# One masked product per group of tiles, and beta by ScalarE: the inverse of a gated DeltaNet layer

## The chip, the cores and the metric

The kernel runs on one core of one Trainium2 chip. The metric is the device time of one execution in microseconds (us); of several runs the median counts. In the profile PE is TensorE, the matmul engine (PEld its weight loads), DVE is VectorE, ACT is ScalarE, POOL is GpSimd, and SP is SyncE, which issues DMAs.

## What is computed

Two layers of a trunk run over 640 tokens: a gated MLP (layer A) and then a bidirectional gated DeltaNet (layer B) with 8 heads of 128 key and 256 value channels. The change is in layer B. Cut to what matters, for a head and a direction:

```python
diff  = gcum[..., :, None] - gcum[..., None, :]
decay = jnp.exp(jnp.where(tril_incl, diff, -jnp.inf))
kb    = kc * bc[..., None]                       # bc is beta, one number per token
A     = jnp.where(tril_strict, einsum('bnhid,bnhjd->bnhij', kb, kc) * decay, 0.0)
lhs   = A + jnp.eye(CHUNK_B)
sol   = triangular_solve(lhs, rhs, left_side=True, lower=True)
qk    = jnp.where(tril_incl, einsum('bnhid,bnhjd->bnhij', qc, kc) * decay, 0.0)
...
v_new = u_i - w_i @ S                            # scan over the chunks
o     = qd_i @ S + qk_i @ v_new
S     = S * gl_i + kd_i.T @ v_new
```

So A is the decayed Gram matrix of the keys, times beta of a row, under a strict triangular mask; the unit matrix plus A is inverted. The query-key matrix with its inclusive mask is multiplied with the solution. Both are done once forward and once backward, and the two directions differ in their triangular masks and in beta.

## The kernel before

Layer B takes the 640 tokens as 5 tiles of 128 (tile 0 the context, tiles 1 to 4 the latents), and its chunk is a tile of 128. The inverse is made by `chunk`, for one head and one group of tiles at a time: `GROUPS = (0,), (1, 4), (2, 3)`, so nt is 1, 2 and 2. There are 8 heads, 24 calls, 40 tiles, and 80 pairs of a tile and a direction.

A call of `chunk` does this. L964 multiplies keys and queries with the keys on PE into a PSUM bank; L967 and L969 (DVE) multiply by the decay `ex`, into g (`ge` in the profile) and pe. L974 makes A: for each tile and direction one DVE operation on 128x128 elements, g times beta (one number per partition) times the strict mask m[0] or m[1]. After the next `yield` L982 makes two of the four parts of M in the same way, from pe and the inclusive masks m[2] and m[3]; L985 (ACT) writes the key parts of M, `kn` scaled by one number per partition. L988 and L990 (POOL) split A plus the unit matrix into two 16-bit halves, A16 and L16; L1002 (PE) turns A16, L1004 (DVE) and L1005 (POOL) write the first level of the inverse into the tile TU; then come six levels (L1017 PE, L1022 DVE, L1028 and L1029 PE, L1032 ACT), a step that refines the inverse (L1047 to L1066), and L1073 (PE) multiplies M by it. L1075 (ACT) copies the product into G, which the scan of this head reads later (L1125, L1126).

A and M have one buffer for each nt. Group (2,3) therefore writes M only when L1073 of group (1,4) has read its own, and that is shortly before its own L1073, when the kernel goes over from one head's scan to the next.

The work of a head is cut into parts (projection, convolution, z gate, `scan`, `chunk` of the next head, norm, residual), each a generator that is advanced from `yield` to `yield` in the order of due times (`stages`, `turns`). With `tc.manual_schedule(engines=MANUAL)` PE and SP keep the order in which this writes their instructions. On DVE, ACT and POOL the order is the scheduler's. Every engine runs its own queue in order: one that waits holds all behind it.

Around the change stand, on the same engines: the short convolution of the next head, L845 (ACT), four L848 (DVE), tanh L851 (ACT), L853 (DVE), and then L240 (PE), which transposes its result into the one PSUM bank of kind `px` that L938 (ACT) reads out and frees; the z gate L1199 (ACT) and L1200 (DVE), which free a bank of kind `pp`; the scan L1112 (PE), L1115 (DVE), L1118 (ACT), L1131 and L1138 (ACT), L1140 (DVE), which adds up the output o and frees a bank of kind `ps` that L1112 fills next; and the split of weights into two parts, L230 (ACT) and L231 (POOL or DVE). PSUM banks: pp 2, pt 3, px 1, ps 2.

Of the kernel before, what the change touches and what calls it, by code (L numbers as in the profile page):

```python
# [9 lines left out]
AF = mybir.ActivationFunctionType  # L10
ALU = mybir.AluOpType
PSUM = bass.MemoryType.PSUM

P = 128
# [193 lines left out]
class Trunk:  # L208
# [8 lines left out]
    def t(self, pool, shape, dt, tag, bufs=None):  # L217
        kw = {} if bufs is None else {"bufs": bufs}
        return pool.tile(shape, dt, tag=tag, name=self.name(tag), **kw)
# [724 lines left out]
    def chunk(self, h, cs):  # L944


        nc, a, t = self.nc, self.a, self.t
        b1, b2 = self.b1, self.b2
        m = self.masks
        kq = self.kq[h]  # L950
        nt = len(cs)
# [3 lines left out]
        two_each = lambda ap: ap[:, :, None, :].broadcast_to([P, 2, nt, P])  # L955
# [10 lines left out]
        g = t(b1, [P, nt, P], F32, f"ge{nt}", bufs=AB[nt - 1])  # L966
        nc.vector.tensor_tensor(g, pg[:, 0], self.ex[:, those], op=ALU.mult)  # L967
        pe = t(b1, [P, nt, P], F32, f"pe{nt}")
        nc.vector.tensor_tensor(pe, pg[:, 1], self.ex[:, those], op=ALU.mult)  # L969

        A = t(b1, [P, 2, nt, P], F32, f"A{nt}", bufs=AB[nt - 1])
        for i, c in enumerate(cs):
            for d in range(2):
                nc.vector.scalar_tensor_tensor(A[:, 1 - d, i], g[:, i], self.beta[:, c, d, h : h + 1], m[:, 1 - d],  # L974
                                               op0=ALU.mult, op1=ALU.mult)

        M = t(b1, [P, nt, 4, P], F32, f"M{nt}")
        keys = lambda c, d: c == 0 or c != (4, 1)[d]
        yield
        for i, c in enumerate(cs):  # L980
            for d in range(2):
                nc.vector.scalar_tensor_tensor(M[:, i, 1 + d], pe[:, i], self.beta[:, c, d, h : h + 1], m[:, 2 + d],  # L982
                                               op0=ALU.mult, op1=ALU.mult)
                if keys(c, d):
                    nc.scalar.activation(M[:, i, 3 * d], kn[:, i], AF.Copy, scale=self.scal[:, 2 + d, c, h : h + 1])  # L985
        yield
        A16 = t(b1, [P, 2, nt, P], F16, f"A16{nt}", bufs=A16B[nt - 1])
        nc.gpsimd.tensor_tensor(A16, A, self.ident[:, None, None, :].broadcast_to([P, 2, nt, P]), op=ALU.add)  # L988
        L16 = t(b1, [P, 2, nt, P], F16, f"L16{nt}", bufs=A16B[nt - 1])
        nc.gpsimd.tensor_tensor(L16, A, A16, op=ALU.subtract)  # L990
        yield
# [429 lines left out]
```

## Time and profile before

| | before |
|---|---|
| median of 3 runs | 1355.61 us (1353.62 to 1361.57) |
| profiled execution, its own time | 1356.03 us |
| its span | 1354.2 us |
| granted TensorE clock, mean | 0.99 |
| layer A | 0 to about 540 us |
| layer B, projection of the first head to the last scan | about 540 to 1240 us |
| output of layer B | about 1240 to 1354 us |

The span is what the profiler saw between the first and the last instruction. A line such as `L974 DVE ... A<-ge,beta,masks 128x128 ... x80 | 28.6, 415 | 0.0` tells line 974, engine, operation, what is written from what, partitions by elements, how many, then their busy time in us, the mean of one in ns, and the engine's idle time just ahead of them. In a timeline the row begins with start and duration in us, and the bracket at its end is the idle time ahead of it and who ended it. A waits row gives total, times and the longest in us.

### The profile page before, as it was taken

Reading aid. Unit: us, or ns where it says so; the run is one execution under the profiler, and the core shown is the slowest. Engines: PE = TensorE matmul, PEld = TensorE weight load, DVE = VectorE, ACT = ScalarE, POOL = GpSimd, SP = SyncE. Lnnn points to the kernel's source line nnn. Section 1 sums busy time; section 2 is a strip of 40 time slices with the busy share of each in tenths; the row PEclk is TensorE's granted clock in tenths of the full one; section 3 lists DMA queues with packets and bytes.
Section 4 is the critical chain, followed back from the end, with each engine's and each line's share of the span. In section 5 each row is a group of like instructions: output and inputs, shape, how many; then the busy total and the mean of one; then the engine's idle time right before and its main releaser. Section 6 shows DMA issues by size and latency. Waiting matters only on the chain. (4 is left out here: it accounts for less than half of the span.)

```text
span 1354.2 us, 22812 instructions
## 1 busy us (share of the span) xinstructions
PE 1282.5 (95%) x8773; PEld 1137.3 (84%) x8773; DVE 875.7 (65%) x1655; ACT 578.7 (43%) x1352; POOL 502.0 (37%) x503
## 2 busy tenths in 40 slices
PE   7999999999999999888999999999999999999996
PEld 4688999999997887778888898999899898887785
DVE  4654744444447566798677778686787868656357
ACT  2333522222224334665545354564545546443320
POOL 0221422222223434354343536355464646520024
PEclk9999999999999999998999999999999999999999
DMA  8512233333336324142122422234233242445732
GB/s 337 168 63 93 94 125 125 125 125 125 125 125 218 118 76 145 56 140 86 50 77 73 136 78 65 100 89 153 79 125 108 85 139 88 133 141 174 261 117 78
DMA packets 90254, 163.17 MB, mean 120 GB/s; under 512 B 9089, under 2 KB 55457, under 8 KB 90017
## 3 DMA queue, kind: packets, MB, share of 16 engines
q1 hardware_dynamic: 88704, 156.99, 35.3%
q10 hardware_dynamic: 1440, 4.72, 1.0%
q8 instruction: 69, 1.13, 0.3%
q14 instruction: 41, 0.33, 0.1%
HBM read 135.97 MB, written 25.71 MB: 119 GB/s over the span
## 5 line engine op out<-in xcount | busy, mean ns | idle before, releaser
L231 POOL TENSOR_TENSOR wlo<-wraw,whi 128x256 fp32r<-128x256 f32 (+1 forms) x188 | 194.4, 1054 | 261.6 <-ACT whi L230 261.6
L235 PE MATMUL pp<-hThi,whi 128*128 128x320 f32 (+1 forms) x784 | 280.1, 357 | 0.2 <-ACT hThi L230 0.2
L237 PE MATMUL pp<-hTlo,whi 128*128 128x320 f32 (+1 forms) x784 | 244.7, 312 | 0.4 <-POOL hTlo L231 0.4
L236 PE MATMUL pp<-hThi,wlo 128*128 128x320 f32 (+1 forms) x784 | 244.1, 311 | 0.0
L230 ACT CAST whi<-wraw 128x256 fp32r<-128x256 f32 (+1 forms) x262 | 143.5, 593 | 84.6 <-PE pacc L236 57.6
L235 PE MATMUL pacc<-hThi,whi 128*128 128x320 f32 x512 | 159.6, 312 | 0.0
L237 PE MATMUL pacc<-hTlo,whi 128*128 128x320 f32 x512 | 158.3, 309 | 0.0
L236 PE MATMUL pacc<-hThi,wlo 128*128 128x320 f32 x512 | 158.2, 309 | 0.0
L848 DVE SCALAR_TENSOR_TENSOR cacc<-xp,convw,cacc 128x642 f32<-128x642 f32 x128 | 137.7, 1076 | 25.0 <-ACT cacc L845 23.6
L235 PEld LDWEIGHTS pp<-hThi,whi 128*128 128x128 f32 (+1 forms) x784 | 148.8, 190 | 3.9 <-ACT hThi L230 0.3
L236 PEld LDWEIGHTS pp<-hThi,wlo 128*128 128x128 f32 (+1 forms) x784 | 148.6, 190 | 4.0
L237 PEld LDWEIGHTS pp<-hTlo,whi 128*128 128x128 f32 (+1 forms) x784 | 147.7, 188 | 1.8 <-POOL hTlo L231 0.7
L231 DVE TENSOR_TENSOR wlo<-wraw,whi 128x1024 fp32r<-128x1024 f32 (+1 forms) x74 | 87.7, 1196 | 60.0 <-ACT whi L230 59.5
L248 POOL TENSOR_TENSOR rs<-ve,mhalf 128x1 f32<-128x1 f32 (+2 forms) x39 | 40.1, 1028 | 170.1 <-DVE ve L246 166.7
L235 PEld LDWEIGHTS pacc<-hThi,whi 128*128 128x128 f32 x512 | 96.1, 188 | 3.1 <-issue 2.2
L236 PEld LDWEIGHTS pacc<-hThi,wlo 128*128 128x128 f32 x512 | 96.1, 188 | 0.0
L237 PEld LDWEIGHTS pacc<-hTlo,whi 128*128 128x128 f32 x512 | 96.1, 188 | 0.0
L256 POOL TENSOR_SCALAR gsq<-gsq 128x320 f32<-128x320 f32 (+1 forms) x52 | 27.7, 532 | 138.4 <-ACT gsq L255 137.4
L257 DVE TENSOR_TENSOR gsq<-pacc,gsq 128x320 f32<-128x320 f32 (+1 forms) x52 | 29.1, 565 | 73.9 <-POOL gsq L256 73.8
L255 ACT ACTIVATE gsq<-pacc 128x320 f32<-128x320 f32 (+1 forms) x52 | 25.7, 498 | 106.2 <-PE pacc L237 102.3
L235 PE MATMUL pacc<-whi,hThi 128*128 128x512 f32 x160 | 63.1, 406 | 7.6 <-ACT whi L230 4.4
L1032 ACT CAST TU<-pt 128x512 f16<-128x512 f32 (+1 forms) x120 | 57.2, 525 | 26.4 <-PE pt L1029 25.5
(333 smaller groups left out, 2974.9 us busy)
## 6 DMA issues: line engine op xcount, KB each, us to landing
wraw<-in_w_b SPq DMA_DIRECT2D x48, 512.0 KB
wraw<-in_w_ada SPq DMA_DIRECT2D x37, 512.0 KB
wraw<-in_w_uz SPq DMA_DIRECT2D x32, 512.0 KB
v<-kvd SPq DMA_DIRECT2D x72, 128.0 KB
wraw<-in_a_wo SPq DMA_DIRECT2D x16, 512.0 KB
wraw<-in_b_wo SPq DMA_DIRECT2D x16, 512.0 KB
kvd<-nat SPq DMA_DIRECT2D x24, 320.0 KB
cacc<-yd SPq DMA_DIRECT2D x24, 320.0 KB
```

The lines of the kernel that those rows point to most:

```text
L230: self.nc.scalar.copy(hi, src)
L231: (e_lo or self.nc.vector).tensor_tensor(lo, src, f32(hi), op=ALU.subtract)
L235: mm(out, l_hi, r_hi, start=start, stop=False)
L236: mm(out, l_lo, r_hi, start=False, stop=False)
L237: mm(out, l_hi, r_lo, start=False, stop=stop)
L248: nc.gpsimd.tensor_tensor(r, ve, self.mhalf[:, 0:n], op=ALU.pow)
L255: nc.scalar.activation(sq, u, AF.Square)
L256: nc.gpsimd.tensor_scalar(sq, sq, GB, 1.0, op0=ALU.mult, op1=ALU.add)
L257: nc.vector.tensor_tensor(sq, u, sq, op=ALU.mult)
L848: nc.vector.scalar_tensor_tensor(acc, xp[:, i : i + PADN], w[:, i : i + 1], acc, op0=ALU.mult, op1=ALU.add)
L1032: nc.scalar.copy(part, p.rearrange("p s k t (j b) -> p s (k t j) b", b=b))
```

## The change

A: one DVE operation multiplies g by both strict masks for all tiles of the group (128x256 elements for nt = 1, 128x512 for nt = 2), and then ACT multiplies each tile and direction by its beta, in place. M: the same with pe, the inclusive masks and the two middle parts of M. 160 DVE operations on 128x128 elements go; 48 DVE operations (16 with 256 and 32 with 512 elements) and 160 ACT operations on 128x128 elements come. Lines behind stand one further down (L985 becomes L986, L1004 L1005, L1140 L1141).

```diff
         A = t(b1, [P, 2, nt, P], F32, f"A{nt}", bufs=AB[nt - 1])
+        nc.vector.tensor_tensor(A, g[:, None].broadcast_to([P, 2, nt, P]), two_each(m[:, 0:2]), op=ALU.mult)
         for i, c in enumerate(cs):
             for d in range(2):
-                nc.vector.scalar_tensor_tensor(A[:, 1 - d, i], g[:, i], self.beta[:, c, d, h : h + 1], m[:, 1 - d],
-                                               op0=ALU.mult, op1=ALU.mult)
+                nc.scalar.activation(A[:, 1 - d, i], A[:, 1 - d, i], AF.Copy, scale=self.beta[:, c, d, h : h + 1])
 
         M = t(b1, [P, nt, 4, P], F32, f"M{nt}")
         keys = lambda c, d: c == 0 or c != (4, 1)[d]
         yield
+        nc.vector.tensor_tensor(M[:, :, 1:3], pe[:, :, None, :].broadcast_to([P, nt, 2, P]),
+                                m[:, None, 2:4, :].broadcast_to([P, nt, 2, P]), op=ALU.mult)
         for i, c in enumerate(cs):
             for d in range(2):
-                nc.vector.scalar_tensor_tensor(M[:, i, 1 + d], pe[:, i], self.beta[:, c, d, h : h + 1], m[:, 2 + d],
-                                               op0=ALU.mult, op1=ALU.mult)
+                nc.scalar.activation(M[:, i, 1 + d], M[:, i, 1 + d], AF.Copy, scale=self.beta[:, c, d, h : h + 1])
                 if keys(c, d):
                     nc.scalar.activation(M[:, i, 3 * d], kn[:, i], AF.Copy, scale=self.scal[:, 2 + d, c, h : h + 1])
```

PE's order is the same up to the last scan; the orders of DVE and ACT change in more than the edited rows. In the rows below the names carry buffer numbers, and x4 is a run of four alike.

DVE, group (1,4) of the first head (607 to 614 us of the trace), before:

```order
L967 TENSOR_TENSOR ge_890_5560<-pt_5542,ex_5475 128x256
L969 TENSOR_TENSOR pe_891_5562<-pt_5542,ex_5475 128x256
L974 SCALAR_TENSOR_TENSOR A_892_5564<-ge_890_5560,beta_4873,masks_4857 128x128 x4
L853 SCALAR_TENSOR_TENSOR cacc_5473<-xp_766_4887,cacc_5473 128x642
L982 SCALAR_TENSOR_TENSOR M_893_5569<-pe_891_5562,beta_4873,masks_4857 128x128
L859 MEMSET xp_766_4887 128x2
L982 SCALAR_TENSOR_TENSOR M_893_5569<-pe_891_5562,beta_4873,masks_4857 128x128 x3
L1004 TENSOR_TENSOR TU_896_5585<-pt_5586,wm_756_4859 128x2x128
```

The same place with the change:

```order
L967 TENSOR_TENSOR ge_890_5562<-pt_5544,ex_5475 128x256
L969 TENSOR_TENSOR pe_891_5564<-pt_5544,ex_5475 128x256
L972 TENSOR_TENSOR A_892_5566<-ge_890_5562,masks_4857 128x512
L853 SCALAR_TENSOR_TENSOR cacc_5473<-xp_766_4887,cacc_5473 128x642
L980 TENSOR_TENSOR M_893_5572<-pe_891_5564,masks_4857 128x2x256
L859 MEMSET xp_766_4887 128x2
L1005 TENSOR_TENSOR TU_896_5588<-pt_5589,wm_756_4859 128x2x128
```

Four operations each of A and of M became one, and two of M's no longer stand on either side of the MEMSET ahead of TU.

DVE at the first change of heads (674 to 683 us), where group (1,4) of the second head meets its convolution; cacc is the convolution's sum, o the scan's output. Before:

```order
L967 TENSOR_TENSOR ge_1078_6513<-pt_6503,ex_6452 128x256
L848 SCALAR_TENSOR_TENSOR cacc_6450<-xp_766_4887,convw_4867,cacc_6450 128x642
L969 TENSOR_TENSOR pe_1079_6515<-pt_6503,ex_6452 128x256
L848 SCALAR_TENSOR_TENSOR cacc_6450<-xp_766_4887,convw_4867,cacc_6450 128x642
L974 SCALAR_TENSOR_TENSOR A_1080_6517<-ge_1078_6513,beta_4873,masks_4857 128x128 x4
L853 SCALAR_TENSOR_TENSOR cacc_6450<-xp_766_4887,cacc_6450 128x642
L1140 TENSOR_TENSOR o_6469<-o_6469,ps_6509 128x256
L859 MEMSET xp_766_4887 128x2
L982 SCALAR_TENSOR_TENSOR M_1081_6522<-pe_1079_6515,beta_4873,masks_4857 128x128 x4
L1004 TENSOR_TENSOR TU_1084_6539<-pt_6540,wm_756_4859 128x2x128
```

With the change:

```order
L967 TENSOR_TENSOR ge_1078_6521<-pt_6511,ex_6458 128x256
L848 SCALAR_TENSOR_TENSOR cacc_6456<-xp_766_4887,convw_4867,cacc_6456 128x642
L969 TENSOR_TENSOR pe_1079_6523<-pt_6511,ex_6458 128x256
L848 SCALAR_TENSOR_TENSOR cacc_6456<-xp_766_4887,convw_4867,cacc_6456 128x642
L972 TENSOR_TENSOR A_1080_6525<-ge_1078_6521,masks_4857 128x512
L848 SCALAR_TENSOR_TENSOR cacc_6456<-xp_766_4887,convw_4867,cacc_6456 128x642
L1141 TENSOR_TENSOR o_6475<-o_6475,ps_6517 128x256
L980 TENSOR_TENSOR M_1081_6531<-pe_1079_6523,masks_4857 128x2x256
L1005 TENSOR_TENSOR TU_1084_6549<-pt_6550,wm_756_4859 128x2x128
L853 SCALAR_TENSOR_TENSOR cacc_6456<-xp_766_4887,cacc_6456 128x642
L859 MEMSET xp_766_4887 128x2
```

The last L848 moved behind A's product, and L853, which ends the convolution, moved from ahead of o, M and TU to behind them.

ACT at the same change of heads (667 to 671 us), from the first G copy to the convolution's first step L845. Before:

```order
L1075 COPY G_1051_6405<-pt_6406 128x384
L985 ACTIVATE M_914_5665<-kn_905_5635,scal_4871 128x128 x4
L1075 COPY G_1051_6405<-pt_6434 128x384
L834 COPY xp_766_4887<-pp_6378 128x320
L230 CAST whi_6670<-wraw_6311 128x256
L845 ACTIVATE cacc_6450<-xp_766_4887,convw_4867 128x642
```

With the change:

```order
L1076 COPY G_1051_6411<-pt_6412 128x384
L986 ACTIVATE M_914_5670<-kn_905_5639,scal_4871 128x128 x3
L984 ACTIVATE M_914_5670<-M_914_5670,beta_4873 128x128 x4
L986 ACTIVATE M_914_5670<-kn_905_5639,scal_4871 128x128
L1076 COPY G_1051_6411<-pt_6440 128x384
L834 COPY xp_766_4887<-pp_6384 128x320
L975 ACTIVATE A_1067_6483<-A_1067_6483,beta_4873 128x128
L845 ACTIVATE cacc_6456<-xp_766_4887,convw_4867 128x642
```

M's four scalings stand between the key parts of M, one of A's two ahead of L845, and a weight cast moved to behind it.

ACT in a later head, around the copy L938 that frees the px bank (998 to 1002 us is such a place). Before:

```order
L938 ACTIVATE nat_7574<-px_7575 128x512
L1118 ACTIVATE o_7584<-ps_7585,scal_4871 128x256
L1118 ACTIVATE o_7588<-ps_7589,scal_4871 128x256
L1032 CAST TU_1311_7538<-pt_7642 128x2x64x2
L1199 ACTIVATE z_1315_7564<-pp_7567 128x320
L938 ACTIVATE nat_7574<-px_7657 128x128
```

With the change:

```order
L938 ACTIVATE nat_7590<-px_7591 128x512
L1119 ACTIVATE o_7600<-ps_7601,scal_4871 128x256
L1119 ACTIVATE o_7604<-ps_7605,scal_4871 128x256
L975 ACTIVATE A_1332_7631<-A_1332_7631,beta_4873 128x128 x4
L1200 ACTIVATE z_1315_7580<-pp_7583 128x320
L1033 CAST TU_1311_7553<-pt_7660 128x2x64x2
L938 ACTIVATE nat_7590<-px_7675 128x128
L1200 ACTIVATE z_1315_7580<-pp_7677 128x320
```

A's four scalings stand ahead of the z gate's, TU's and px's copies, and the z gate's has moved ahead of TU's.

## The prediction

> **What bounds the kernel now.** I read the page first, then the busy time by stage, then TensorE's waits in the stage that the change touches, then the groups of the changed lines, and last the stretches of the timeline around TensorE's longest waits.
>
> ```profile
> span 1354.2 us, 22812 instructions
> PE 1282.5 (95%) x8773; PEld 1137.3 (84%) x8773; DVE 875.7 (65%) x1655; ACT 578.7 (43%) x1352; POOL 502.0 (37%) x503
> ```
>
> TensorE (PE) is busy for 95% of the span. The edited lines run in layer B alone, so its heads are what counts. A row below has a stretch, its length, then busy time and instructions of PE, weight loads, DVE, ACT and POOL, and the granted clock.
>
> ```profile
> 560.00:620.00 60.00, 49.57 (x301) 44.04 (x300) 56.65 (x89) 38.19 (x114) 33.74 (x29) 0.94 0.33 102
> 980.00:1040.00 60.00, 59.30 (x475) 55.22 (x473) 45.02 (x94) 29.16 (x83) 38.20 (x44) 1.00 0.34 111
> ```
>
> Two regimes: while the first head is prepared (560 to 620 us) DVE is busy 56.65 of 60 us and PE idles 10.4; in a steady head PE idles 0.7 of 60. DVE work taken away is worth nothing where PE has 59.30 of 60 us of its own to do. What can be won stands in PE's waits for DVE between 560 and 1240 us (total, times, longest, in us):
>
> ```profile
> PE px L240 <- DVE cacc L853: 8.0, 4, 4.4
> PE pt L1017 <- DVE TU L1004: 4.1, 2, 2.6
> PE ps L1112 <- DVE o L1140: 3.9, 5, 1.2
> PE pt L1073 <- DVE T L1066: 2.0, 2, 1.2
> ```
>
> These four, 18.0 us together, are the waits whose producer stands near the edited lines on DVE. They bound the gain: 1356.0 - 18.0 = 1338.
>
> **What goes and what comes.** Groups (busy us, mean ns, idle before them):
>
> ```profile
> L974 DVE SCALAR_TENSOR_TENSOR A<-ge,beta,masks 128x128 f32<-128x128 f32 x80 | 28.6, 415 | 0.0
> L982 DVE SCALAR_TENSOR_TENSOR M<-pe,beta,masks 128x128 f32<-128x128 f32 x80 | 50.8, 685 | 2.6 <-PE pt L1073 2.1
> L985 ACT ACTIVATE M<-kn,scal 128x128 f32<-128x128 f32 x64 | 21.4, 393 | 13.5 <-DMA kn<-kvd 8.0 <-PE pt L1073 5.5
> L967 DVE TENSOR_TENSOR ge<-pt,ex 128x256 f32<-128x256 f32 x16 | 6.7, 418 | 1.3 <-PE pt L964 0.6
> ```
>
> DVE loses 28.6 + 50.8 = 79.4 us. It gets 32 products of 512 elements and 16 of 256. No product by a mask of just this form is in the trace; the nearest rows are a two-operand product of 512 at 0.69 us with POOL idle (594.86 below) and L967 at 0.42. So 32 x 0.69 + 16 x 0.42 = 28.8 us, and DVE nets -51. ACT gets 160 scalings of the size of L985. Alone one takes 0.39 us; four in a row take 1.28 (980.34 below), a pitch of 0.30. That is 160 x 0.32, about 51 us. ACT is busy 29.16 of 60 us in a steady head, so the load fits (8 heads, 6.4 us more for each). Whether it stands in somebody's way is decided place by place.
>
> **Place 1, the first head.** Start, duration, engine, line; in brackets the idle time before and who ended it.
>
> ```profile
> 594.86 0.69 DVE L796 TENSOR_TENSOR grhs<-masks,ghi 128x512 fp32r<-128x512 f32 x1
> 600.13 0.82 DVE L982 SCALAR_TENSOR_TENSOR M<-pe,beta,masks 128x128 f32<-128x128 f32 x1
> 602.16 0.76 DVE L982 SCALAR_TENSOR_TENSOR M<-pe,beta,masks 128x128 f32<-128x128 f32 x1
> 607.21 1.13 DVE L974 SCALAR_TENSOR_TENSOR A<-ge,beta,masks 128x128 f32<-128x128 f32 x4
> 608.26 0.82 DVE L853 SCALAR_TENSOR_TENSOR cacc<-xp,cacc 128x642 f32<-128x642 f32 x1
> 609.00 2.60 DVE L982 SCALAR_TENSOR_TENSOR M<-pe,beta,masks 128x128 f32<-128x128 f32 x2
> 611.52 2.28 DVE L982 SCALAR_TENSOR_TENSOR M<-pe,beta,masks 128x128 f32<-128x128 f32 x2
> 613.72 0.41 DVE L1004 TENSOR_TENSOR TU<-pt,wm 128x256 f16<-128x256 f32 x1
> 608.42 1.79 POOL L988 TENSOR_TENSOR A<-A,ident 128x512 f16<-128x512 f32 x1 [2.48 <-DVE A L974]
> 610.29 1.16 POOL L990 TENSOR_TENSOR L<-A,A 128x512 f16<-128x512 f32 x1
> 609.13 0.66 PE L240 MATMUL px<-ident,cacc 128*128 128x128 f32 x4 [2.49 <-DVE cacc L853]
> 614.18 0.26 PE L1017 MATMUL pt<-TU,A 128*128 128x64 f16 x2 [2.60 <-DVE TU L1004]
> ```
>
> PE stops twice: for the convolution's last step (L853), then for TU (L1004). Both producers stand on DVE behind edited work. Ahead of L853, A's four operations take 1.13 us and become one of 0.69 (-0.4), and M's pair of group (0,), which the scheduler had put between the convolution's steps, at 0.82 + 0.76 becomes one of 0.42 (-1.2): **-1.6** of the 2.49. Ahead of L1004 stand M's four operations, 4.9 us from 609.00 to 613.8, though L974 shows four at 1.13 with little POOL work beside them. Each of them ends about when a POOL operation ends (610.2, 611.5): the two engines take turns, and four short operations lose four turns. One product loses at most one. I take 0.69 when it finds POOL idle and 0.69 + 1.79 behind the longest POOL row here; so it ends at 609.7 to 611.5, and L1004 at 610.1 to 611.9, where PE comes at 611.6 (614.18 - 2.60); what L853 gains moves both alike. The stop shrinks to between 0 and 0.3, and I take **-2.6**.
>
> The Trainium skill, "SBUF — State Buffer", section "Who interferes with whom", says that a VectorE instruction with two SBUF inputs contends with a GpSimd instruction that reads SBUF, and that whoever comes second is fully blocked. The rows of place 1 agree (1.2 us each instead of 0.28). It speaks against a full win too, for the new product also has two SBUF inputs; by it the term would be the -2.3 of the worse end.
>
> **Place 2, the first change of heads.**
>
> ```profile
> 667.66 1.28 ACT L985 ACTIVATE M<-kn,scal 128x128 f32<-128x128 f32 x4 [1.99 <-PE pt L1073]
> 669.82 0.84 ACT L845 ACTIVATE cacc<-xp,convw 128x642 f32<-128x642 f32 x1
> 671.72 2.58 DVE L848 SCALAR_TENSOR_TENSOR cacc<-xp,convw,cacc 128x642 f32<-128x642 f32 x2
> 675.83 1.01 DVE L848 SCALAR_TENSOR_TENSOR cacc<-xp,convw,cacc 128x642 f32<-128x642 f32 x1
> 676.93 0.74 ACT L851 ACTIVATE xp<-cacc 128x642 f32<-128x642 f32 x1 [2.42 <-DVE cacc L848]
> 678.27 0.82 DVE L853 SCALAR_TENSOR_TENSOR cacc<-xp,cacc 128x642 f32<-128x642 f32 x1
> 679.15 1.11 PE L240 MATMUL px<-ident,cacc 128*128 128x128 f32 x4 [4.44 <-DVE cacc L853]
> ```
>
> This is one chain: L845 on ACT opens the next head's convolution, four L848 follow on DVE, tanh (L851) on ACT, L853 on DVE, and PE stops for it. M of group (2,3) is rewritten in the same moment, and now its four scalings stand on ACT ahead of L845, with one of A's; a weight cast, which I count like one scaling, moves from ahead of L845 to behind it: 4 x 0.30 = 1.2 us. L845 ended at 670.7 and L848 began only at 671.7, when DVE was free of A and M; so 1.0 of the 1.2 is covered, and the convolution starts 0.2 late. A's product of 0.69 now stands ahead of the fourth L848, which ends at 676.8 + 0.2 + 0.7 = 677.7. Behind it the new order has the o sum (L1140, of L1004's size, so 0.41), M's product (0.69, or 1.79 if it meets POOL) and L1004 (0.41) ahead of L853. L851 runs beside these. L853 can start at 679.2 to 680.3 instead of 678.27: +0.9 to +2.0, and I take **+1.3**, nearer to a product that finds POOL idle. If the three operations were hidden behind L851 altogether it would be +0.2.
>
> **Place 3, the steady heads.** PE's five waits of L1112 for the o sum come from L1140 standing on DVE behind two of M's operations, slowed as in place 1 (993.44 below; PE's wait ends there when L1140 is through). With one product in their place those 3.9 us go. In exchange, ACT gets four A scalings ahead of the copy that frees the one px bank:
>
> ```profile
> 993.44 2.61 DVE L982 SCALAR_TENSOR_TENSOR M<-pe,beta,masks 128x128 f32<-128x128 f32 x2
> 999.73 1.61 DVE L974 SCALAR_TENSOR_TENSOR A<-ge,beta,masks 128x128 f32<-128x128 f32 x4
> 1001.99 0.27 ACT L938 ACTIVATE nat<-px 128x128 f32<-128x128 f32 x1
> 1002.45 0.60 PE L240 MATMUL px<-ident,o 128*128 128x128 f32 x4
> 1001.96 1.28 POOL L988 TENSOR_TENSOR A<-A,ident 128x512 f16<-128x512 f32 x1
> 980.34 1.28 ACT L985 ACTIVATE M<-kn,scal 128x128 f32<-128x128 f32 x4 [0.74 <-PE pt L1073]
> 983.94 1.02 PE L1073 MATMUL pt<-M,T 128*128 128x256 f32 x4
> ```
>
> The product ends at 999.73 + 0.69 = 1000.4, the scalings at 1001.7; then come the z copy, the TU copy and L938, about 1.0 us as before, so px is free at 1002.7 instead of 1002.3, and PE wants it at 1002.45: a new stop of about 0.4, in five heads 2.0. A itself is ready at 1001.7 and POOL takes it at 1001.96, so A's own delay is hidden. At the change of heads M is complete after eight ACT operations, 980.34 + 0.39 + 7 x 0.30 = 982.8, and PE wants it at 983.94: hidden, with 1.1 us to spare. Net **-1.9**; bounds -3.9 (no new stop) and, with the full 1.28 exposed five times, +2.5.
>
> **Place 4, the last head.**
>
> ```profile
> 1153.49 0.66 PE L240 MATMUL px<-ident,cacc 128*128 128x128 f32 x4 [0.75 <-DVE cacc L853]
> 1157.77 0.22 PE L1017 MATMUL pt<-TU,A 128*128 128x64 f16 x2 [1.45 <-DVE TU L1004]
> ```
>
> The same pair of stops as in place 1, 2.2 us together, behind four A and four M operations; I take **-1.9**, leaving 0.3 for the scalings. The last wait of L1073 for T (1.2 us at most) has M's operations on DVE ahead of it: **-0.4**. In the tail the order of SyncE's loads differs a little; 0, within 2 either way.
>
> **Sum.** -1.6 - 2.6 + 1.3 - 1.9 - 1.9 - 0.4 = -7.1 on the profiled execution's 1356.0 (its span of 1354.2 and 1.8 around it, which stay), so 1348.9. That execution lies 0.4 above the median of 1355.6; against the median, and that is the forecast, 1348.5.
>
> **Rivals.** (a) *ACT's queue becomes the late one: slower.* An ACT operation waiting for a DVE product holds everything behind it: the copies of px, pp and G. The place is ACT around L938 and around L1075/L845. If one burst of four (1.28) is exposed at both places in each of seven later heads, 17.9 us are added; less the waits that go (1.6 + 2.6 + 3.9 + 2.2 = 10.3) that gives 1363.6. It decides from where PE's slack behind an ACT copy is under 1.28 us; at L938 it is 0.2, which speaks for it; at L1073 1.1 are left after the change and the A chain is hidden, which speaks against it. I give it 0.18.
>
> The Trainium skill, "ScalarE: Activation LUTs", "Rules for kernel authors", says to put multiplications on VectorE and not on ScalarE. That is a rule against this change, and rival (a) is what it would cost here. The rows (0.30 us at pitch for ACT, 0.28 for DVE's four with POOL quiet) show no dearer operation on ACT, so only the place in the queue speaks for it.
>
> (b) *The waits only move.* PE keeps its written order; what it does not wait for at 609 and 614 it waits for at the next TU, behind POOL's three operations, and px eats the 3.9. What remains is place 4's 2.2 and place 2's loss, -2.2 + 1.3: 1355.1. The first head's DVE at 56.65 of 60 speaks for it in part; that 4.9 us of DVE go against it. 0.22.
>
> (c) *All of the waits go.* 18.0 less 2.0 at px: 1340.0. For it: each wait has an edited operation within a few rows. Against it: the order at place 2, which moves L853 back. 0.17.
>
> The forecast has 0.43. Measurement tells changes over 0.5% (6.8 us) from none, and my sum lies on that line; I put 0.25 of it on the faster side. Faster: 0.25 + 0.17 = 0.42; same: 0.18 + 0.22 = 0.40; slower: 0.18. The range reaches from (c), 1340, to (a), 1363.
>
> **What would show it.** PE's stop at about 614 us gone and the one at 609 under 1 us; the one at 679 at 5.3 to 6.4 us; no wait of L1112 for L1140, and waits of L240 for L938 of about 0.4 instead; DVE busy 51 us less, ACT 51 more. I am wrong if PE's waits for ACT in the steady heads exceed 6 us together, or if DVE's new products mostly take over 1.5 us.

## The result and the profile after

| | before | with the change |
|---|---|---|
| median of 19 runs each | 1355.61 us | 1363.17 us (1360.17 to 1370.04) |
| ratio to before | | 1.0055, 95% interval 1.0044 to 1.0065 |
| profiled execution, span | 1354.2 us | 1364.8 us |

The change makes the kernel 0.55% slower: 7.6 us by the medians, where 7.1 us less were forecast. Rival (a), ACT's queue as the late one, had been worked out to 1363.6; how it came to that number is taken up below. The profiled execution (1366.5 us) is one of the longer ones, so its stretches add up to some 3 us more than the medians.

The page of the changed kernel, its span and its busy times:

```profile
span 1364.8 us, 22886 instructions
PE 1286.6 (94%) x8773; PEld 1140.5 (84%) x8773; DVE 837.7 (61%) x1543; ACT 624.2 (46%) x1512; POOL 505.0 (37%) x503
```

DVE is busy 38.0 us less (875.7 to 837.7), ACT 45.5 more (578.7 to 624.2). PE does the same work and has more idle time. Its waits between 560 and 1240 us:

```profile
PE px L240 <- ACT nat L938: 11.3, 6, 2.3
PE px L240 <- DVE cacc L853: 7.3, 3, 5.7
PE pt L1029 <- DVE Y L1023: 6.1, 6, 2.0
```

The waits for TU at L1017 (4.1) are gone, and of those for the o sum at L1112 (3.9) 0.2 are left. But there are six new waits for L938, the copy that frees the px bank, 11.3 us together, and those of L1029 for Y (L1028 before) have grown from 1.8 to 6.1. The stretches of before again, in us of the longer span:

```profile
560.00:620.00 60.00, 51.32 (x328) 45.86 (x327) 55.71 (x84) 44.29 (x134) 34.10 (x29) 1.00 0.35 108
980.00:1040.00 60.00, 57.01 (x447) 53.44 (x448) 38.15 (x79) 33.19 (x98) 36.59 (x42) 1.00 0.35 112
```

The first head has won a little (PE 49.57 to 51.32). A steady head, which had nothing to win, has lost: 59.30 to 57.01 of 60 us, though DVE is nearly 7 us freer in it.

One steady wait, followed back. Timeline rows of SP, ACT, DVE and PE in one head of the changed kernel:

```profile
834.15 3.75 SPq L1133 DMA_DIRECT2D out_new_state<-r  x2
836.00 1.28 ACT L975 ACTIVATE A<-A,beta 128x128 f32<-128x128 f32 x4 [1.60 <-DVE xp L859]
837.19 0.35 ACT L1132 COPY r<-ps 128x256 f32<-128x256 f32 x1
838.43 0.92 SPq L1098 DMA_DIRECT2D v<-kvd  x2
842.42 0.48 DVE L1116 SCALAR_TENSOR_TENSOR r<-ps,neg,v 128x256 f32<-128x256 f32 x1 [2.86 <-DMA v<-kvd]
844.07 0.68 DVE L972 TENSOR_TENSOR A<-ge,masks 128x512 f32<-128x512 f32 x1
844.85 1.28 ACT L975 ACTIVATE A<-A,beta 128x128 f32<-128x128 f32 x4 [0.79 <-DVE A L972]
846.60 0.28 ACT L938 ACTIVATE nat<-px 128x128 f32<-128x128 f32 x1
846.93 0.66 PE L240 MATMUL px<-ident,o 128*128 128x128 f32 x4 [1.80 <-ACT nat L938]
```

The scalings of A of group (1,4) stand in ACT's queue ahead of the second copy of the new state (L1132). SP has to store that copy before it may go on, so its two stores take from 834.15 to 837.9, and the loads of v behind them start at 838.43. On DVE the scan's L1116 waits 2.86 us for v, and the next group's A product (L972) stands behind it. A's next scalings on ACT wait for the product, L938 waits behind the scalings, and PE behind L938. (The bracket of the row at 836.00 names L859, a DVE operation beside the A product that the scalings read.) Before, the same places read:

```profile
831.51 0.96 SPq L1132 DMA_DIRECT2D out_new_state<-r  x2
831.65 0.38 ACT L1131 COPY r<-ps 128x256 f32<-128x256 f32 x1
833.01 0.93 SPq L1097 DMA_DIRECT2D v<-kvd  x2
837.93 0.87 DVE L1115 SCALAR_TENSOR_TENSOR r<-ps,neg,v 128x256 f32<-128x256 f32 x2
839.81 1.13 DVE L974 SCALAR_TENSOR_TENSOR A<-ge,beta,masks 128x128 f32<-128x128 f32 x4
842.07 0.27 ACT L938 ACTIVATE nat<-px 128x128 f32<-128x128 f32 x1
842.52 0.60 PE L240 MATMUL px<-ident,o 128*128 128x128 f32 x4
```

The second copy ran at 831.65, the two stores took 0.96 us, not 3.75, v was there when L1115 came, and PE did not wait for L938. In all heads DVE waited for v 1.0 us in one place before; now:

```profile
DVE r L1116 <- DMA v<-kvd: 18.6, 7, 3.7
```

### The profile page after: what moved, and what is told of

Read it like the earlier page. It is cut to its first block, busy times and chain, and to the rows that moved or that the text cites. A ratio compares the mean times of both kernels' runs of the same rounds, so it can differ in the third digit from the quotient of the medians.

```text
span 1364.8 us, 22886 instructions
## 1 busy us (share of the span) xinstructions
PE 1286.6 (94%) x8773; PEld 1140.5 (84%) x8773; DVE 837.7 (61%) x1543; ACT 624.2 (46%) x1512; POOL 505.0 (37%) x503
## 5 line engine op out<-in xcount | busy, mean ns | idle before, releaser
L231 POOL TENSOR_TENSOR wlo<-wraw,whi 128x256 fp32r<-128x256 f32 (+1 forms) x188 | 196.0, 1064 | 246.1 <-ACT whi L230 232.4
L848 DVE SCALAR_TENSOR_TENSOR cacc<-xp,convw,cacc 128x642 f32<-128x642 f32 x128 | 135.1, 1056 | 33.9 <-ACT cacc L845 32.4
L231 DVE TENSOR_TENSOR wlo<-wraw,whi 128x1024 fp32r<-128x1024 f32 (+1 forms) x74 | 89.4, 1219 | 63.3 <-ACT whi L230 63.0
```

What stands on the lines that cost most here:

```text
L231: (e_lo or self.nc.vector).tensor_tensor(lo, src, f32(hi), op=ALU.subtract)
L848: nc.vector.scalar_tensor_tensor(acc, xp[:, i : i + PADN], w[:, i : i + 1], acc, op0=ALU.mult, op1=ALU.add)
```

## The experiments

The theory has two links: scalings of group (1,4) hold the second state copy, and by it SP, v and DVE (link 1); scalings of group (2,3) hold L938 (link 2). Link 2 alone is the 0.4 us of the prediction; with link 1 it would be the 1.8 of the row above. The rivals: M's scalings, the new products and their order on DVE, or ACT's burst alone. Every kernel ran in turns with the kernel before, whose median there was 1354.9 to 1357.0.

| | median, us | ratio to before, 95% interval |
|---|---|---|
| only A | 1359.56 | 1.0023 (1.0006 to 1.0040) |
| only M | 1352.07 | 0.9972 (0.9960 to 0.9983) |
| stores by ACT | 1349.40 | 0.9955 (0.9943 to 0.9968) |
| scaling on DVE | 1381.79 | 1.0181 (1.0155 to 1.0208) |
| before, stores by ACT | 1362.38 | 1.0042 (1.0025 to 1.0059) |
| late stores | 1351.83 | 0.9965 (0.9952 to 0.9979) |
| A of (2,3) as before | 1353.86 | 0.9976 (0.9960 to 0.9993) |
| A of (1,4) as before | 1352.86 | 0.9973 (0.9958 to 0.9987) |
| before, late stores | 1354.78 | 0.9994 (0.9976 to 1.0011) |
| late stores, A of (2,3) as before | 1348.49 | 0.9949 (0.9931 to 0.9967) |
| only M, late stores | 1348.06 | 0.9949 (0.9930 to 0.9967) |
| late stores, two buffers of A | 1351.46 | 0.9966 (0.9951 to 0.9982) |

### Only A, only M

```diff
 # only A: M's lines of the change undone
-        nc.vector.tensor_tensor(M[:, :, 1:3], pe..., m[:, None, 2:4, :]..., op=ALU.mult)
-                nc.scalar.activation(M[:, i, 1 + d], M[:, i, 1 + d], AF.Copy, scale=self.beta[...])
+                nc.vector.scalar_tensor_tensor(M[:, i, 1 + d], pe[:, i], self.beta[...], m[:, 2 + d], ...)
 # only M: A's lines of the change undone in the same way
```

> Only A is made the new way (one masked product, four scalings on ACT); M is as before. Theory: the time is lost by A's scalings on ACT, which hold the second copy of the new state, by it SP's loads of v, DVE and then the copy that frees px. Then PE's waits of L240 for L938 stay at about 1.8 us in six heads, M's four operations keep their waits on DVE, and the time is 1362 to 1369 us. Rival, the loss comes with M's scalings at the change of heads: then this kernel is within 1350 to 1356.

> Only M is made the new way; A is as before. Theory (A's scalings lose the time): PE's stop at 614 us and the waits of L1112 for the o sum go, no wait of L240 for L938 over 0.5 us comes, and the time is 1346 to 1353 us. Rival (M's scalings lose it): 1360 us or more, with waits for ACT around L1074 or L240.

Only A is slower, though by less than expected (1359.6 against 1362 at the least), with the waits of the theory; two rows, of PE's and of DVE's waits:

```profile
PE px L240 <- ACT nat L938: 9.0, 6, 1.8
DVE r L1115 <- DMA v<-kvd: 20.1, 8, 4.7
```

Only M is faster, has no wait of L240 for L938, and lies within what the theory gave. So it is A's half that loses and M's half that wins, and the whole change (+7.6) is worse than the sum of its halves (+4.1 and -3.4 against the runs of before beside them). Why the halves do not add up was not tested.

### Link 1 cut in two ways, with a control for each

```diff
 # stores by ACT
-                    nc.sync.dma_start(self.o["new_state"][d, h], s2)
+                    nc.scalar.dma_start(self.o["new_state"][d, h], s2)
 # late stores (another kernel): still on SP, behind the next step's loads of v
-                    nc.sync.dma_start(self.o["new_state"][d, h], s2)
+                    late.append((d, s2))
...
                 units.append(unit(c, d, kv))
+            for d, s2 in late:
+                nc.sync.dma_start(self.o["new_state"][d, h], s2)
+            late.clear()
```

> The whole change, but the two stores of the new state of each head are issued by ACT, right behind their copies, instead of by SP, so SP no longer waits for them ahead of its loads of v. Theory (the size of the px wait comes through SP and v): DVE's waits for v go from 18.6 to under 4 us, A's product comes about 2 us earlier, PE's wait of L240 for L938 falls from 1.8 to 0 to 0.6 us per head, and the time is 1351 to 1357 us. Rival (four scalings in ACT's queue cost this much by themselves): the waits stay at 1.5 us or more and the time at 1361 to 1365.

> The whole change, the stores still on SP, but written behind the loads of v of the next step. It cuts the same link as the stores on ACT did and adds nothing to ACT. Theory (SP waiting for the store ahead of v is what sets the size of the px wait): DVE waits for v under 5 us in all, PE's wait of L240 for L938 about 0.4 us in the steady heads, 1347 to 1353 us. Rival (what helped was ACT's queue with the stores in it, or how the scheduler then laid it out): 1358 to 1364 us.

Both are faster than the change, by 13.8 and 11.3 us, and DVE's wait for v does not appear in either. Late stores lie in the theory's range, stores by ACT below it (1349.4, where 1351 was the least). In five heads the stop for L938 is 0.5 us with late stores and 0.4 with stores by ACT, as the theory has it; in the last head it is still 1.2 and 1.5, so there late v is not what makes most of it. The same place in the kernel with late stores, SP, DVE, ACT and PE:

```profile
827.23 1.03 SPq L1098 DMA_DIRECT2D v<-kvd  x2
828.86 3.74 SPq L1164 DMA_DIRECT2D out_new_state<-r  x2
836.48 1.16 DVE L972 TENSOR_TENSOR A<-ge,masks 128x512 f32<-128x512 f32 x1
837.73 1.28 ACT L975 ACTIVATE A<-A,beta 128x128 f32<-128x128 f32 x4 [1.56 <-DVE A L972]
839.49 0.28 ACT L938 ACTIVATE nat<-px 128x128 f32<-128x128 f32 x1
839.82 0.66 PE L240 MATMUL px<-ident,o 128*128 128x128 f32 x4 [0.47 <-ACT nat L938]
```

SP still waits 3.74 us at its stores, but now v is on its way. A's scalings still stand ahead of L938, and PE's stop is 0.47 instead of 1.80: link 2 alone.

The controls put the same edits into the kernel before:

> Control: the kernel before, with the two stores of the new state of a head issued by ACT instead of SP and nothing else. Theory (the store costs only where A's scalings hold the copy ahead of it; before, SP waited for it about 1 us): 1353 to 1357 us, no difference from before. Rival (the place of the stores is worth 5 to 6 us by itself, and the change is worth nothing): 1348 to 1351 us.

> Second control: the kernel before, with the stores of the new state written behind the next step's loads of v, still on SP. In the kernel before v came in time, so theory: 1353 to 1358 us, waits of PE as before (L1112 for the o sum about 4 us). Rival (the place of the stores is worth 4 us or more by itself): 1348 to 1351 us.

Late stores change nothing that shows in the kernel before (0.9994; the interval reaches down to 3 us less), so of the 11 us most are the link's and not the stores'. Stores by ACT make the kernel before slower by 0.42%, which neither the theory nor its rival gave. Its row says where:

```profile
PE ps L1112 <- DVE o L1140: 9.7, 5, 2.3
```

The wait for the o sum went from 3.9 to 9.7: DVE there does all four of M's operations ahead of L1140, where it did three before. What made the scheduler choose so was not tried. For the changed kernel, late stores are therefore the cleaner of the two tests.

### One link at a time

```diff
 # A of group (2,3) as before; the other kernel has GROUPS[1], which is (1,4)
+        if cs != GROUPS[2]:
             nc.vector.tensor_tensor(A, g..., two_each(m[:, 0:2]), op=ALU.mult)
...
+                if cs != GROUPS[2]:
                     nc.scalar.activation(A[:, 1 - d, i], A[:, 1 - d, i], AF.Copy, scale=self.beta[...])
+                else:
+                    nc.vector.scalar_tensor_tensor(A[:, 1 - d, i], g[:, i], self.beta[...], m[:, 1 - d], ...)
```

> The whole change except in group (2,3), whose A is made as before on DVE; so no scalings stand on ACT ahead of L938, while those of group (1,4) still stand ahead of the second copy of the new state. Theory (two links, SP's loads of v and the scalings ahead of L938, and PE stops only at the end of both): DVE still waits for v some 18 us in all, but PE's wait of L240 for L938 is under 0.3 us per head, and the time is 1350 to 1356 us. Rival (late v alone costs the time, whoever reads it next): 1360 us or more.

> The whole change except in group (1,4), whose A is made as before on DVE; so the second copy of the new state has no scalings ahead of it, while those of group (2,3) still stand ahead of L938. Theory: DVE waits for v under 5 us in all, PE's wait of L240 for L938 about 0.4 us per head, the time 1348 to 1354 us. Rival (the scalings ahead of L938 alone are the price): waits of 1.5 us or more and 1359 us or more.

Both times lie within what the theory gave. With A of (2,3) as before, v is as late as in the change, and PE waits for L938 only 0.4 us in one place, the last head:

```profile
DVE r L1121 <- DMA v<-kvd: 18.7, 7, 3.4
```

So late v alone does not make PE's stop; it does because scalings behind it stand ahead of L938. Whether late v costs something besides is not settled: with late stores added (below) this kernel goes from 0.9976 to 0.9949, and the two intervals just overlap. With A of (1,4) as before the wait for v falls to 3.2 us in all, and PE's wait for L938 to 1.5 in two places, in all less than expected, though 1.2 of it is in the last head. In the first five of the six stops the links are in series: cutting either one takes most of the wait.

### Is ACT the wrong engine for the scaling?

```diff
-                nc.scalar.activation(A[:, 1 - d, i], A[:, 1 - d, i], AF.Copy, scale=self.beta[...])
+                nc.vector.tensor_scalar(A[:, 1 - d, i], A[:, 1 - d, i], self.beta[...], None, op0=ALU.mult)
 # and the same for M
```

> Both masked products as in the change, but all 160 scalings by beta are done in place on DVE and none on ACT. Theory (ACT's queue loses the time): no wait of L240 for L938 above 0.5 us, DVE is busy 30 to 50 us longer than in the change, its old waits (L1112 for the o sum, TU at 614 us) come back in part, and the time is 1350 to 1358 us. Rival (the new product or the order on DVE loses it): 1361 us or more.

The wait for L938 goes, as expected, but the time was far off: 1381.8, the slowest of all, where the theory gave 1350 to 1358 and the rival (the new product or the order on DVE) 1361 or more. PE's waits for DVE take over; for TU the kernel before had 4.1 us:

```profile
PE pt L1018 <- DVE TU L1005: 12.4, 7, 2.3
```

DVE is busy 894.3 us, 57 more than in the change, where 30 to 50 were expected; the scalings cost it 382 ns each for A and 619 for M. The profiled execution (1375.0 us) is shorter than the median; of its 19 us over the one before, 8.3 are these waits for TU and another 8.3 PE's busy time (1290.8 us, mean clock 0.986; before 1282.5 and 0.990). So the time does not speak for the rival: late stores kept the new products on DVE and PE's stop of 5.7 us at the first change of heads, and came out faster than the kernel before. What this kernel shows is the price of 160 more operations on DVE. The Trainium skill, "ScalarE: Activation LUTs", section "Rules for kernel authors", puts multiplications on VectorE. By that rule this kernel should beat the change; here it is 18.6 us behind it. Here the operations that stand behind the scalings in a queue mattered more than the engine that multiplies.

### Versions that go further

> Both links cut: the whole change with late stores, and A of group (2,3) made as before on DVE. Theory (the links are in series, so cutting the second gains only what the first left, 3.6 us of waits): PE's wait of L240 for L938 under 1 us in all, DVE's waits for v under 5 us, 1346 to 1352 us. Rival (each link costs by itself): 1343 to 1346 us.

> Only M the new way, with late stores. Theory: M alone gave 1352 and had 7.4 us of waits of DVE for v, nearly all off PE's path, so 1349 to 1353 us and no difference from M alone that shows. Rival (late v cost M alone as well): 1345 to 1348 us.

Each is built from edits shown above. Both beat the kernel before by 0.5% and the change by over 14 us. The first came as the theory had it, with no wait for L938 in the list; it is not told apart from late stores alone (intervals overlap). The second fell between the theory and its rival, and its interval (0.9930 to 0.9967) overlaps that of M alone (0.9960 to 0.9983): whether late v costs M alone something stays open. A gain of A's half beyond M's half, then, shows in no run.

```diff
-AB, A16B, TUB, YB, NB, GB_ = (1, 1), (1, 2), (1, 2), (1, 2), (1, 1), (2, 4)
+AB, A16B, TUB, YB, NB, GB_ = (1, 2), (1, 2), (1, 2), (1, 2), (1, 1), (2, 4)
```

> The whole change with late stores, and two buffers of A and g for groups of two tiles instead of one. Theory for the first head (the stop of PE at 615 us, 2.0 us for Y, is the old stop at 614 moved: DVE's product of the next A waits 1.4 us for POOL's last reading of the one buffer, with Y queued behind it): no wait of DVE's A product for POOL, PE's stop there at 0 to 0.7 us, 1348 to 1352 us, so 1 to 2 us under late stores alone. Rival (Y is late for another reason, POOL's turns with DVE): the stop stays at 1.5 us or more and the time at 1351 to 1353.

This is for the first head. In the change DVE's product for group (2,3) waits 1.39 us for POOL's last reading of A's one buffer, Y stands behind it, and PE stops 2.04 us; DVE and PE rows:

```profile
608.90 0.66 PE L240 MATMUL px<-ident,cacc 128*128 128x128 f32 x4 [1.32 <-DVE cacc L853]
613.38 1.63 DVE L972 TENSOR_TENSOR A<-ge,masks 128x512 f32<-128x512 f32 x1 [1.39 <-POOL L L991]
614.93 0.28 DVE L1023 TENSOR_TENSOR Y<-pt,wm 128x128 f16<-128x128 f32 x1
615.26 0.23 PE L1029 MATMUL pt<-Y,TU 128*128 128x64 f16 x2 [2.04 <-DVE Y L1023]
```

With two buffers the product starts at once and that stop is gone; but PE stops at the next Y's:

```profile
612.06 0.86 DVE L972 TENSOR_TENSOR A<-ge,masks 128x512 f32<-128x512 f32 x1
612.84 0.28 DVE L1023 TENSOR_TENSOR Y<-pt,wm 128x128 f16<-128x128 f32 x1
619.74 0.22 PE L1029 MATMUL pt<-Y,TU 128*128 128x64 f16 x2 [0.72 <-DVE Y L1023]
621.56 0.27 PE L1029 MATMUL pt<-Y,TU 128*128 128x64 f16 x2 [1.54 <-DVE Y L1023]
```

The time is that of late stores alone (1351.5 and 1351.8), and it lies in the theory's range and in its rival's. The cause of the stop was right, its worth was not: in the first head the waits mostly move.

## Why the prediction was wrong

**What bounds the kernel** held: PE's waits decide, and 38 us less of DVE bought nothing by themselves. Between 560 and 1240 us these waits together went from 37.8 to 43.5 us, and PE's busy time in the whole span from 1282.5 to 1286.6 for the same 8773 matmuls (mean clock 0.990 and 0.988): 9.8 of the 10.5 us between the two profiled executions. The first of the prediction's own signs of being wrong came as well: in the five steady heads PE's waits for ACT's copy are 9.0 us, where 6 was the limit.

**Place 1** was half right. The stop at 609 fell from 2.49 to 1.32 (-1.2 for the -1.6 forecast; the A product there took 1.25 us, not 0.69, beside POOL). The product, and the stop of place 2:

```profile
606.85 1.25 DVE L972 TENSOR_TENSOR A<-ge,masks 128x512 f32<-128x512 f32 x1
679.12 1.12 PE L240 MATMUL px<-ident,cacc 128*128 128x128 f32 x4 [5.69 <-DVE cacc L853]
```

The stop at 614 went (-2.6, as forecast), but 2.0 came back at 615, as rival (b) had it.

**Place 2** was right: the stop at 679 is 5.69, forecast 5.3 to 6.4, with L853 behind o, M and TU as the order has it.

**Place 3 is where it failed**, in one sentence: "The product ends at 999.73 + 0.69 = 1000.4". That kept the start of A's product where it was before. The rest of the step was right: the waits for the o sum went (3.9 to 0.2), scalings and copies follow as listed, and with link 1 cut the stop is 0.4 to 0.5 us, the 0.4 forecast. But the product itself came 1.7 us late against PE (it began 1.06 us ahead of the moment from which PE stood waiting, 844.07 and 845.13 in the rows above; before, 2.7 us ahead of L240, 839.81 and 842.52), by a way through ACT, SP and a DMA that the prediction never looked at: it costed A's scalings of group (1,4) only by what A's own readers would see, and not by what stands behind them in ACT's queue, the second copy of the new state, and behind its store in SP's. The term was 5 x 0.4 and measured 5 x 1.8 = 9.0. The sixth stop, in **place 4**, is 2.3 where 0.3 were left for it, so that place gained nothing of its 1.9; there the scalings ahead of L938 are the larger part, for the stop is 1.2 with link 1 cut and 0.4 with link 2 cut. The term for T, -0.4, came out at -0.8: L1074 waits 1.6 us less for T and 0.8 for M.

With the stops set right, -7.1 becomes -7.1 + 7.0 (place 3) + 2.0 (place 4) + 0.4 + 2.0 (place 1) - 0.4 (T) = +3.9. The medians show +7.6. The waits of L1029 for Y that came elsewhere (0.6 and 0.9 at 622 us, 0.6 at 761) and the clock, below, are of the size of the rest; this division was read from one execution and not tested.

**DVE's and ACT's sums** had the right sign: DVE is 38.0 us less busy (forecast 51) and ACT 45.5 more (forecast 51). The largest groups of the new operations:

```profile
L972 DVE TENSOR_TENSOR A<-ge,masks 128x512 f32<-128x512 f32 x16 | 16.0, 1001 | 1.4 <-POOL L L991 1.4
L980 DVE TENSOR_TENSOR M<-pe,masks 128x512 f32<-128x512 f32 x16 | 12.2, 765 | 2.6 <-PE pt L1074 2.1
L975 ACT ACTIVATE A<-A,beta 128x128 f32<-128x128 f32 x80 | 26.9, 392 | 15.6 <-DVE A L972 9.2 <-DVE xp L859 6.4
```

The products of 512 took 1.00 and 0.77 us instead of 0.69, and all products 36.6 us instead of 28.8, some of them beside POOL (the one at 606.85 beside L231). That is what the Trainium skill, "SBUF — State Buffer", section "Who interferes with whom", leads one to expect of two SBUF inputs. A's scalings cost ACT 26.9 us; the 15.6 us of idle time ahead of them is the price that the prediction left out: an engine that stands waiting with other work behind.

**The chances.** Rival (a), at 0.18, named the right engine and queue, and its 1363.6 is close by luck: its price (1.28 at two places of seven heads, with all the old waits gone) is not what happened. At the change of heads nothing was exposed to speak of (one wait of L1074 for M, 0.8 us), at L938 it was 1.8 and came by way of SP and v, and waits for Y came back.

## What to carry to other kernels

When work moves to an engine with room, follow every instruction that the new operations are put in front of to its readers, DMA stores too: a queue that issues loads and stores in order passes one late copy on to all loads behind it. Where a store may wait for a producer, write it behind the loads that somebody waits for; here that alone turned +0.55% into -0.35%. Take the part that stands in nobody's way (here M's half) and leave the other.

## What was not expected of the hardware

Behind some of PE's new stops the granted clock fell. The 5 us after four of the six stops of the changed kernel, PE busy first and the clock third from the end:

```profile
846.90:851.90 5.00, 4.97 (x36) 4.66 (x37) 2.52 (x8) 0.00 (x0) 2.87 (x3) 1.00 0.55 174
764.40:769.40 5.00, 5.00 (x28) 4.77 (x29) 1.69 (x5) 0.00 (x0) 2.82 (x3) 0.66 0.32 101
927.40:932.40 5.00, 4.93 (x28) 4.71 (x29) 1.75 (x5) 0.01 (x1) 3.98 (x4) 0.66 0.55 147
1169.40:1174.40 5.00, 4.76 (x25) 4.25 (x26) 1.63 (x4) 1.91 (x5) 3.62 (x4) 0.66 0.73 236
```

The 0.66 is a mean; from 765 to 767 us the clock was 0.50. In the two slow steady heads PE did 28 matmuls where it did 36 at 1.00, and came to the scan's next L1113 11.0 us after the stop instead of 9.4, some 1.5 us later. So a stop of 1.8 us can cost 3.3, an estimate from these figures. With late stores, where those stops are 0.5 us (1.2 in the last head), the clock stayed at 1.00 behind all six; but so it did behind the six stops of 1.2 to 1.8 us with only A, and in a steady head of the kernel before it fell behind one of 0.83:

```profile
1053.82 0.40 PE L1047 MATMUL pt<-id,U 128*128 128x128 f16 x4 [0.83 <-ACT U L1038]
1055.00:1057.00 2.00, 2.00 (x9) 1.91 (x8) 0.43 (x2) 0.00 (x0) 1.66 (x3) 0.50 0.00 0
```

No length of a stop from which the clock falls can be read from these runs. The Trainium skill, "TensorE: Matmul & The Clock Gate", section "Part 1: The HAM clock gate (the "warmup" mystery)", has the clock fall after an idle window of about 3.4 us that runs free of the kernel. Here it fell behind stops of 0.83 to 2.32 us. That stops alike in length differ in it agrees with a free-running window; the length does not.
